# A hybrid diffusion block on one core: the 16-to-32 step of block inversions on 32x32 tiles, and delta-net decays from two single-pass products

## The chip, the cores and the metric

The kernel runs on one NeuronCore of a Trainium2 chip. A core has TensorE (PE in the profile; PEld is its loading of weights), VectorE (DVE), ScalarE (ACT), GpSimd (POOL) and SyncE (SP, which here issues DMAs). Each engine works through its own queue of instructions in order and waits on semaphores for the others. Matrix products read SBUF and write PSUM, which has eight banks here divided into pools. The metric is the device time of one execution in microseconds (us); lower is better. The time before is the median of three runs.

## The reference, cut to what matters

One layer of a backbone: 256 latent tokens and 256 context tokens, 2048 channels. Modulated RMSNorm, one wide input projection, then two token mixers side by side, RWKV-7 and a chunked gated DeltaNet, each in both directions; their outputs are projected, gated, merged and added; then a SwiGLU feed-forward part. Two pieces bear on the change. The delta net computes in each chunk of 64 tokens

```python
gc = jnp.cumsum(chunks(g), axis=-1)
diff = gc[..., :, None] - gc[..., None, :]
decay = jnp.where(incl, jnp.exp(jnp.where(incl, diff, 0.0)), 0.0)
lmat = jnp.where(strict, jnp.einsum('nbhik,nbhjk->nbhij', kb, kc) * decay, 0.0)
sol = lax.linalg.triangular_solve(lmat, rhs, left_side=True, lower=True, unit_diagonal=True)
q_dec = qc * jnp.exp(gc)[..., None]
```

so that each head and direction needs a matrix of exponentials of differences of cumulated log decays, the exponentials of the cumulated decays themselves, and the solution of a unit triangular system of 64 rows. The RWKV recurrence is written in the reference as a scan over single tokens; the kernel computes it in chunks of 64 too, which leads to triangular matrices of the same kind.

## The kernel before, in words

The program has four parts. First, a start phase: norms of both token sets, part of the modulation, and the low-rank projections. Second, the middle, which holds both mixers. Third, the projections of both branches and the merge; fourth, the feed-forward part and the final norm. Parts three and four are long rows of weight products. A weight product in full precision is made of three fp32r (single-pass) products of split operands: ScalarE casts a weight tile to fp32r (`whi`), VectorE subtracts to get the rest (`wlo`), and TensorE multiplies high by high, high by low and low by high. These three are the groups `mm<-hxh,whi`, `mm<-hxl,whi` and `mm<-hxh,wlo`.

The middle isn't written out in order. A planner, `Weave`, takes generators (one per piece of work: `prepare`, `grams`, `inverse`, `values`, `scan` for each of 8 pairs of RWKV heads; `features`, `tokens`, `decays`, `head_grams`, `head_inverse`, `head_scan` for each of 8 delta-net heads; `products` for the input projections; `ada_rest` for further modulation), gives each operation a cost (`Lane`), and emits the operations in the order in which its own clock lets them start, by rank among those that are ready. Named marks (`yield "scan", p - 1` and the like) hold a piece back until another has been reached. The emitted order is then each engine's queue order. `products` has a low rank and fills TensorE where nothing else is ready. Since every operation is issued from one line, L142 stands for all of the middle in the profile, and groups are told apart by tile names.

An inversion (`invert`) works on `nu` unit triangular blocks of 64x64 per half of the partitions: 16 for an RWKV pair (8 chunks, two directions) and 8 for a delta-net head. The blocks go through DRAM (`scr`, `tscr`) into a layout in which VectorE inverts all 16x16 diagonal blocks by substitution. They come back as `T0` and, transposed, `Tx`. Then two merging steps follow on TensorE: 16 to 32 and 32 to 64. The 16-to-32 step goes direction by direction: a product of 64x64 tiles with half the columns (32) into the one bank of the pool `pi`, a masked copy by VectorE (`Qm`, with the mask `qmask`), a second product of the same form, an addition into `T0`, and a transpose to `Tx`. The 32-to-64 step (`quads`) already uses 32x32 tiles. RWKV's `scan` of a pair and the delta net's `head_scan` wait for their inversion.

`decays` makes, per head and direction, an operand `gm` (a triangle of ones times the log decays, 128x512, by VectorE), multiplies it in fp32 by the triangle `aft` (512 columns) and by `ones` (256 columns), and takes exponentials on ScalarE: `Ed`, which GpSimd masks, and `eq`, which VectorE multiplies into `Qe`. `gm` lies in one place of a hand-divided `arena`.

Of the kernel before, what the change touches and what calls it, by code (L numbers as in the profile page):

```python
# [18 lines left out]
P = 128  # L19
# [18 lines left out]
for _name, _w in (("ident", 128), ("ones", 128), ("bd64", 128), ("rmask", 256),  # L38
                  ("qmask", 64), ("tri", 256), ("aft", 256), ("q4", 4), ("q2", 2),
                  ("eps", 1), ("gneps", 1)):  # L40
    _C[_name] = (_n, _n + _w)
    _n += _w
NC_COLS = _n

# [10 lines left out]
def const_array():  # L55
# [12 lines left out]
    rb, cb = s // 16, t // 16  # L68
    same = (rb // 2) == (cb // 2)
    even = np.arange(64) // 16 % 2 == 0  # L70
    put("qmask", np.concatenate([(same & (rb % 2 == 1))[:, even], (same & (rb % 2 == 0))[:, ~even]], 1))
# [39 lines left out]
class Lane:  # L111
# [5 lines left out]
    def __getattr__(self, name):  # L117

        def op(out, *a, **k):
# [148 lines left out]
def emit(ctx: ExitStack, tc, A, out, dbg=None):  # L268
# [17 lines left out]

    C = cst.tile([P, NC_COLS], F32, name="C")
    Q.dma_start(C, A["consts"])
# [12 lines left out]
    ident, ones, bd64 = c_("ident"), c_("ones"), c_("bd64")  # L301
    rmask = c_("rmask").rearrange("p (d k) -> p d k", d=2)
    qmask = c_("qmask").rearrange("p (d a c) -> p d a c", d=2, a=2)
    tri = c_("tri").rearrange("p (d t) -> p d t", d=2)
    aft = c_("aft").rearrange("p (d t) -> p d t", d=2)
# [23 lines left out]
    zero = cst.tile([P, 130], F32, name="zero")  # L329
    G.memset(zero, 0.0)  # L330
# [74 lines left out]
    with tc.tile_pool(name="p0", bufs=1) as p0, \  # L405
            tc.manual_schedule(engines={mybir.EngineType.PE, mybir.EngineType.DVE, mybir.EngineType.Activation,
                                        mybir.EngineType.SP}):
        modc = p0.tile([P, 32], F32, name="modc")
# [143 lines left out]
    def invert(pool, Lt, parts, nu, which, full, fill):  # L552
# [52 lines left out]
        def half(t, d):  # L605
            ax = "p u"[:2 * len(t.shape) - 3]
            return t.rearrange(f"{ax} (a b c) -> {ax} a b c", a=2, b=2)[..., d, :]

        def mm(ps, d, lhs, rhs):
            return [e.matmul(ps[64 * h:64 * h + 64, 32 * i:32 * i + 32], lhs(h, h2 * d + i), rhs(h, h2 * d + i),  # L610
                             start=True, stop=True) for i in range(h2) for h in range(2)]
# [1087 lines left out]
```

## Time and profile before

| | us |
|---|---|
| median of three runs (2334.98 to 2337.48) | 2336.01 |
| the profiled execution | 2348.77 |
| its span, first to last instruction | 2346.7 |
| TensorE busy (95%) | 2223.8 |
| VectorE busy (66%) | 1557.2 |
| ScalarE busy (45%) | 1047.9 |
| GpSimd busy (5%) | 113.5 |

Busy time says that instructions were in flight; matmuls overlap, so a busy TensorE can still be waiting between them, and the distance from one start to the next is the better measure of what a matmul costs. A row of groups gives the line, the engine, the operation, out<-in by tile names, the shapes, the count, then busy us and mean ns of one, then the idle time before it and what ended that. A row of the timeline gives start and length in us; x32 means that 32 records were merged. An fp32 matmul leaves two records, an fp32r matmul one. Rows of busy time by stretch give busy us and count for each engine, then the clock granted to TensorE (1.00 is full), the share of the DMA engines and the rate.

### The profile page before, as it was taken

To read this page: it belongs to the slowest core of one execution; us is meant where nothing else is said; L and a number is where in the kernel's file an instruction comes from. 1 tells how busy PE (TensorE), PEld (TensorE's weight loads), DVE (VectorE), ACT (ScalarE), POOL (GpSimd) and SP (SyncE) were. 2 spreads that over 40 slices of the span, in tenths; PEclk is the share of its full clock that TensorE was granted. 3 is DMA by queue.
4 is the path that set the end of the run, shared out by engine and by line. 5 is a ranking of instruction groups with operands and counts; after the bars stand their busy time and mean duration, and the time that the engine had idled before them with its cause. 6 is when DMAs were issued, how large, how long until landed. Compare 5 with 4: busy or idle time off the path is not lost. (4 is left out here: it accounts for less than half of the span.)

```text
span 2346.7 us, 51488 instructions
## 1 busy us (share of the span) xinstructions
PE 2223.8 (95%) x21368; PEld 1951.7 (83%) x21368; DVE 1557.2 (66%) x3237; ACT 1047.9 (45%) x1863; POOL 113.5 (5%) x183
## 2 busy tenths in 40 slices
PE   7988999999999999999798999999999999999998
PEld 4767677778788777776677989999999999999997
DVE  3447588778986489889878645765666556545454
ACT  3246454544355544344234346544444444444443
POOL 0000000000000011111111003000000000000000
PEclk9999999999999999999789999999999999999999
DMA  9956454434344256657466565663777776566665
GB/s 377 397 148 189 152 134 102 111 83 117 100 109 133 85 172 207 189 167 217 145 191 194 182 219 180 209 214 107 239 233 234 234 238 218 187 185 194 191 191 165
DMA packets 232570, 430.58 MB, mean 183 GB/s; under 512 B 114832, under 2 KB 130064, under 8 KB 227984
## 3 DMA queue, kind: packets, MB, share of 16 engines
q1 hardware_dynamic: 204688, 351.78, 48.4%
q0 software_dynamic: 13824, 50.34, 7.0%
q10 hardware_dynamic: 13824, 25.17, 3.5%
q8 instruction: 167, 2.74, 0.5%
q14 instruction: 67, 0.55, 0.1%
HBM read 401.45 MB, written 25.77 MB: 182 GB/s over the span
## 5 line engine op out<-in xcount | busy, mean ns | idle before, releaser
L357 DVE TENSOR_TENSOR wlo<-wraw,whi 128x1024 fp32r<-128x1024 f32 x328 | 393.5, 1200 | 351.1 <-ACT whi L356 348.2
L356 ACT CAST whi<-wraw 128x1024 fp32r<-128x1024 f32 x328 | 337.7, 1030 | 472.8 <-PE mm L367 413.8
L142 PE MATMUL mm<-hxh,wlo 128*128 128x256 f32 (+1 forms) x1376 | 468.3, 340 | 9.9 <-DVE wlo L142 9.7
L142 PE MATMUL mm<-hxh,whi 128*128 128x256 f32 (+1 forms) x1376 | 469.0, 341 | 3.4 <-ACT whi L142 3.3
L142 PE MATMUL mm<-hxl,whi 128*128 128x256 f32 (+1 forms) x1376 | 468.3, 340 | 0.0
L368 PE MATMUL mm<-hfh,wlo 128*128 128x256 f32 x1344 | 377.1, 281 | 0.4 <-DVE wlo L357 0.4
L366 PE MATMUL mm<-hfh,whi 128*128 128x256 f32 x1344 | 376.5, 280 | 0.0
L367 PE MATMUL mm<-hfl,whi 128*128 128x256 f32 x1344 | 375.2, 279 | 0.0
L142 PEld LDWEIGHTS mm<-hxh,wlo 128*128 128x128 f32 x1376 | 265.6, 193 | 39.4 <-DVE wlo L142 13.0
L142 PEld LDWEIGHTS mm<-hxh,whi 128*128 128x128 f32 x1376 | 265.6, 193 | 31.5 <-issue 6.5
L142 PEld LDWEIGHTS mm<-hxl,whi 128*128 128x128 f32 x1376 | 265.8, 193 | 27.2 <-issue 6.1
L142 DVE TENSOR_TENSOR wlo<-wraw,whi 128x512 fp32r<-128x512 f32 x344 | 236.2, 690 | 62.7 <-ACT whi L142 60.0
L142 ACT CAST whi<-wraw 128x512 fp32r<-128x512 f32 x344 | 205.8, 618 | 112.1 <-PE mm L142 88.9
L366 PEld LDWEIGHTS mm<-hfh,whi 128*128 128x128 f32 x1344 | 253.4, 189 | 0.0
L368 PEld LDWEIGHTS mm<-hfh,wlo 128*128 128x128 f32 x1344 | 252.8, 188 | 0.6 <-DVE wlo L357 0.6
L367 PEld LDWEIGHTS mm<-hfl,whi 128*128 128x128 f32 x1344 | 253.2, 188 | 0.0
L142 DVE TENSOR_TENSOR arena<-arena 128x28 f32<-128x28 f32 (+13 forms) x538 | 132.0, 247 | 32.1 <-DMA arena<-scr 20.4
L366 PE MATMUL mm<-za,whi 128*128 128x256 f32 x512 | 141.8, 277 | 0.0
L367 PE MATMUL mm<-za,whi 128*128 128x256 f32 x512 | 141.7, 277 | 0.0
L368 PE MATMUL mm<-za,wlo 128*128 128x256 f32 x512 | 141.6, 277 | 0.0
L142 DVE SCALAR_TENSOR_TENSOR aw<-aw,ck 128x512 f32<-128x512 f32 x180 | 131.2, 739 | 5.1 <-DMA aw<-ada_rest 4.4
L368 PEld LDWEIGHTS mm<-za,wlo 128*128 128x128 f32 x512 | 96.2, 188 | 0.0
(311 smaller groups left out, 3924.5 us busy)
## 6 DMA issues: line engine op xcount, KB each, us to landing
wraw<-w SPq DMA_DIRECT2D x172, 512.0 KB, 4.3
wraw<-wgu SPq DMA_DIRECT2D x168, 512.0 KB, 4.5
aw<-ada_rest POOLq DMA_DIRECT2D x96, 512.0 KB, 4.7
aw<-ada_first SPq DMA_DIRECT2D x32, 1024.0 KB, 11.5
wraw<-wdn SPq DMA_DIRECT2D x64, 448.0 KB, 3.7
wraw<-wout SPq DMA_DIRECT2D x32, 512.0 KB, 4.7
aw<-ada_gt ACTq DMA_DIRECT2D x64, 256.0 KB, 5.0
wraw<-wdn SPq DMA_DIRECT2D x32, 512.0 KB, 3.6
```

The source lines that it names most:

```text
L142: return Op(self, cost, lambda: getattr(self.engine, name)(out, *a, **k), split)
L356: S.copy(hi[:, c, :M], raw[:, c, :M])
L357: V.tensor_sub(lo[:, c, :M], raw[:, c, :M], hi[:, c, :M].bitcast(F32))
L366: E.matmul(ps, hi, Xh[:, k, :n], start=first and i == 0, stop=False)
L367: E.matmul(ps, hi, Xl[:, k, :n], start=False, stop=False)
L368: E.matmul(ps, lo, Xh[:, k, :n], start=False, stop=last and i == len(wt) - 1)
```

## The change

It has two parts and what they need.

The 16-to-32 step is done for both directions together. Each 32x32 diagonal block is handled by its own tile: a product with the 16 columns that matter, a multiply-add by VectorE per direction (`low16` selects rows, `eye16` adds the identity), a second product of the same form, eight copies into `T0` (four by VectorE, four by ScalarE), and one transpose of all of `T0`. The planner's cost of a matmul with fewer than 64 rows goes from 0.024 to 0.009 or 0.0125.

The log decays are split into an fp32r part `ghi` and the rest `glo`. ScalarE, not VectorE, builds two operands from the triangle, each by four activations with a per-partition scale (128x128). Each product by `aft` and by `ones` becomes two accumulating fp32r products, so `aft` and `ones` are kept as fp32r (`CR`), loaded by a DMA of their own and cast by ScalarE at the start. The exponential is written straight into `Qe` and multiplied there. The operands take the pool places `k` and `kkn` of the RWKV stage, which for that leave the arena; `eq`, `gm`, `q3` and `hb` lose their own places, and `zero` moves to the start phase's pool. Head 0 waits for the inversion of pair 6.

```diff
-                    cost = 0.024
+                    cost = 0.009 if n <= 16 else 0.0125
...
+        cr = p0.tile([P, NR_COLS], F32, name="cr")
+        Q.dma_start(cr, A["consts"][:, NC_COLS - NR_COLS:])
+        S.copy(CR, cr)
...
-        Qm = xt[:, :32 * nu].rearrange("p (u c) -> p u c", c=32)
+        fours = [(h, u, 32 * b, slice(64 * h + 32 * b, 64 * h + 32 * b + 32)) for u in range(nu) for h in range(2) for b in range(2)]
+        Qm = xt[:, :16 * nu].rearrange("p (u c) -> p u c", c=16)
+        ps = yield pib
+        pv = ps[:, 0:32 * nu].rearrange("p (k u c) -> p k u c", k=2, c=16)
+        yield [e.matmul(pv[r, 0, u], Lt(h, u)[b:b + 32, b:b + 32], T0[r, u, b + 16 * (u // h2):b + 16 * (u // h2) + 16],
+                        start=True, stop=True) for h, u, b, r in fours]
         for d in range(2):
-            T0d = half(T0[:, us[d]], d)
-            ps = yield pib
-            yield mm(ps, d, Lt, lambda h, u: half(N_(h, u), d))
-            pv = ps[:, 0:32 * h2].rearrange("p (i a c) -> p i a c", a=2, c=16)
-            yield v.tensor_mul(Qm[:, us[d]].rearrange("p i (a c) -> p i a c", a=2), pv,
-                               qmask[:, d].unsqueeze(1).to_broadcast([P, h2, 2, 16]))
-            yield mm(ps, d, Nt_, lambda h, u: Qm[64 * h:64 * h + 64, u, :])
-            yield v.tensor_add(T0d, pv, T0d)
-            weave.release(pib)
-            yield v.transpose(Tx[:, us[d]], T0[:, us[d]])
+            yield v.scalar_tensor_tensor(Qm[:, us[d]], pv[:, 0, us[d]], low16[:, d:d + 1],
+                                         eye16[:, d].unsqueeze(1).to_broadcast([P, h2, 16]), ALU.mult, ALU.add)
+        yield [e.matmul(pv[r, 1, u], Tx[r, u, b:b + 32], Qm[r, u, :], start=True, stop=True) for h, u, b, r in fours]
+        for h in range(2):
+            yield [(s.copy if h else v.tensor_copy)(T0[r, us[d], b + 16 * d:b + 16 * d + 16], pv[r, 1, us[d]])
+                   for d in range(2) for b in (0, 32) for r in (slice(64 * h + b, 64 * h + b + 32),)]
+        weave.release(pib)
+        yield v.transpose(Tx, T0)
...
+        yield s.copy(ghi, gtok)
+        yield v.tensor_sub(glo, gtok, ghi.bitcast(F32))
...
+        else:
+            yield "inverse", NPAIR - 2
...
-            gm = gs.tile([P, 4, P], F32, tag="gm", name="gm")
-            yield v.tensor_mul(gm, tri[:, d].unsqueeze(1).to_broadcast([P, 4, P]),
-                               gtok[:, :, col:col + 1].to_broadcast([P, 4, P]))
-            gf = gm.rearrange("p b c -> p (b c)")
+            gm = [rpool.tile([P, 512], F32R, tag=t, name="gm") for t in ("k", "kkn")]
+            for t, g2 in zip(gm, (ghi.bitcast(F32), glo)):
+                for b in range(4):
+                    yield s.activation(t[:, P * b:P * b + P], tri[:, d], AF.Identity, scale=g2[:, b, col:col + 1])
             ps = yield pab
-            yield e.matmul(ps, aft[:, d], gf, start=True, stop=True)
+            yield [e.matmul(ps, aftr[:, d], t, start=i == 0, stop=i == 1) for i, t in enumerate(gm)]
...
-            yield e.matmul(ps[:, :T], ones, gf[:, 0:T], start=True, stop=True)
-            eq = gs.tile([P, T], F32, tag="eq", name="eq")
-            yield s.activation(eq, ps[:, :T], AF.Exp)
+            yield [e.matmul(ps[:, :T], onesr, t[:, 0:T], start=i == 0, stop=i == 1) for i, t in enumerate(gm)]
+            qe = o["Qe"][:, d]
+            yield s.activation(qe, ps[:, :T], AF.Exp)
             weave.release(pab)
-            yield v.tensor_mul(o["Qe"][:, d], o["q"], eq)
+            yield v.tensor_mul(qe, qe, o["q"])
...
-        q3 = gs.tile([P, 4, 64], F32, tag="q3", name="q3")
+        q3 = gs.tile([P, 4, 64], F32, tag="XT", name="q3")
```

More of the change, by code (lines that the diff above doesn't have):

```diff
@@ L43 @@
 NC_COLS = _n
+NR_COLS = 384
 _P = {}
@@ L674, in emit @@
     arp = ent(tc.tile_pool(name="arp", bufs=1))
-    arena = arp.tile([P, 9544], F32, name="arena")
-    rplaces = (("k", 512, 1), ("r", T, 1), ("t1", 512, 1), ("kd0", 512, 1), ("kd1", 512, 1), ("kkn", 512, 1), ("sg", 512, 1),
+    arena = arp.tile([P, 8520], F32, name="arena")
+    rplaces = (("r", T, 1), ("t1", 512, 1), ("kd0", 512, 1), ("kd1", 512, 1), ("sg", 512, 1),
                ("ic", 512, 2), ("ei", 520, 1), ("LT", 1024, 2), ("XT", 512, 1), ("prod", 64, 1),
@@ L1130, in emit @@
     nbtok = cst.tile([P, 4, 16], F32, name="nbtok")
+    ghi = cst.tile([P, 4, 16], F32R, name="ghi")
+    glo = cst.tile([P, 4, 16], F32, name="glo")
     al = cst.tile([P, 1], F32, name="al")
@@ L1169, in begin @@
         yield [e.matmul(ps[:, T + 64 * i + 32 * d:T + 64 * i + 32 * d + 32], m[:, d], gtok[:, :, 8 * d:8 * d + 8], start=True, stop=True)
-               for d in range(2) for i, m in enumerate((tri, aft))] + [e.matmul(ps[:, 3 * P:3 * P + 64], ones, gtok, start=True, stop=True)]
+               for d in range(2) for i, m in enumerate((tri, aftr.bitcast(F32)))] + [e.matmul(ps[:, 3 * P:3 * P + 64], ones, gtok, start=True, stop=True)]
         for i, t in enumerate((egc, eta)):
```

48 lines of the change are left out of this document (23 added, 25 removed).

## The prediction

> **What bounds the kernel now.** I read the page's busy line and slices first, then busy time by stretch, the waits of TensorE, the order of time around one inversion and one decay step, and last the groups of instructions by shape.
>
> ```profile
> PE 2223.8 (95%) x21368; PEld 1951.7 (83%) x21368; DVE 1557.2 (66%) x3237; ACT 1047.9 (45%) x1863; POOL 113.5 (5%) x183
> DVE  3447588778986489889878645765666556545454
> ACT  3246454544355544344234346544444444444443
> ```
>
> The shares are averages over unlike stages; the digits show VectorE at 8 or 9 tenths only in the middle. The middle (some 165 to 1390 us) holds both token mixers, and all of the change but its constants lies there.
>
> ```profile
> core 0: us, PE busy (x) PEld busy (x) DVE busy (x) ACT busy (x) POOL busy (x), PEclk, DMA share, GB/s
> 400.00:800.00 400.00, 397.07 (x5220) 312.66 (x5220) 312.60 (x778) 194.93 (x483) 11.24 (x30) 1.00 0.40 107
> 800.00:1000.00 200.00, 186.06 (x1490) 152.36 (x1489) 162.40 (x395) 87.81 (x164) 28.98 (x43) 0.97 0.59 179
> 1000.00:1200.00 200.00, 177.17 (x1380) 138.11 (x1380) 171.37 (x420) 80.53 (x148) 33.48 (x54) 0.90 0.62 186
> 1200.00:1390.00 190.00, 171.99 (x1755) 157.59 (x1755) 134.44 (x349) 78.21 (x162) 11.12 (x17) 0.97 0.59 179
> 1390.00:2346.00 956.00, 929.72 (x7878) 924.12 (x7876) 535.55 (x713) 428.69 (x558) 21.23 (x16) 0.99 0.65 204
> ```
>
> Columns are the stretch, its length, busy time and count of each engine, and the granted clock. In the RWKV stage (400 to 800) TensorE is busy 397 of 400 us at full clock, VectorE 78%, ScalarE 49%. In the delta-net stage (1000 to 1200) TensorE has 89% at a clock of 0.90 and VectorE 86%: two engines near their limit. After 1390 only weight products run (956 us); the change leaves them alone.
>
> ```profile
> PE pa L142 <- DVE arena L142: 0.8, 2, 0.5
> PE mm L142 <- DVE wlo L142: 0.4, 1, 0.4
> PE pa L142 <- ACT arena L142: 5.5, 5, 1.9
> PE pa L142 <- DVE arena L142: 4.0, 2, 3.3
> PE pi L142 <- DMA T<-tscr: 3.3, 1, 3.3
> ```
>
> These are TensorE's waits, total us, times, longest: two rows of 400 to 800, where nothing holds it longer than 0.8 us in all, and three of 1000 to 1200, where the decay products (pa) wait for ScalarE or VectorE. So TensorE time is worth nearly its full amount in the RWKV stage and part of it later.
>
> **Inversion step: the matmuls.** Before, each inversion runs four sets in a row (two directions, two products each), each set on 64x64 tiles, 32 columns wide. Afterwards there are two sets for both directions, of 32x32 tiles and 16 columns. One fp32 matmul is two records in the trace: the RWKV set of 16 matmuls shows as x32.
>
> ```profile
> 622.80 1.12 PE L142 MATMUL pi<-arena 64*64 64x32 f32 x32
> 623.75 0.43 PE L142 MATMUL s<-R,Tx 64*64 64x64 f32 x8
> 625.39 1.12 PE L142 MATMUL pi<-arena,Tx 64*64 64x32 f32 x32
> 626.44 0.45 PE L142 MATMUL s<-VX,KB 128*64 128x64 f32 x8
> 632.40 0.76 PE L142 MATMUL pi<-Tx,arena 32*32 32x32 f32 x64 [0.45 <-DVE arena L142]
> 633.09 0.45 PE L142 MATMUL s<-R,Tx 64*64 64x64 f32 x8
> 1013.31 0.66 PE L142 MATMUL pi<-T,LT 64*64 64x32 f32 x16 [1.00 <-DVE T L142]
> 1024.46 0.45 PE L142 MATMUL pi<-Tx,qo 32*32 32x32 f32 x32
> 1024.84 0.71 PE L142 MATMUL pa<-arena 128*128 128x128 f32 x4
> ```
>
> From start to next start an old RWKV set holds TensorE 0.95 us (622.80 to 623.75) and 1.05 us (625.39 to 626.44), about 1.0. The later 32x32 step, which is kept, is the nearest row for the new form: 64 records in 0.69 us (632.40 to 633.09), some 11 ns a record against 31. A new RWKV set has 64 matmuls, 128 records, half as wide. Upper end: each costs what a 32-column one costs, 2 x 0.69 = 1.38 us. Lower end: half of that, 0.69 us, if the columns count. I take 1.0, between them, since the same tile form is known and only its width is not. So 4 x 1.0 goes and 2 x 1.0 comes: 2.0 us for each of 8 pairs, 16 us (10 to 21).
>
> The Trainium skill ("TensorEngine Tiling (Array Packing)", Performance Considerations, Instruction Overhead) says that a matmul with one column takes as long as one with 60. By it the upper end holds and the RWKV term is 8 x (4.0 - 2.76) = 10 us; no run shown has 16 columns, so the trace neither agrees nor disagrees.
>
> In a delta-net head a set is half as long: the old one lasts 0.66 us, some 0.55 us without the tail that overlaps what follows. A new one has 64 records: 0.69 at most, 0.38 us at least (the x32 run at 1024.46, next start 1024.84); I take 0.55. Four go and two come: 1.1 us for each of 8 heads, 9 us (6.5 to 11.5).
>
> **Inversion step: the other engines.**
>
> ```profile
> L142 DVE TENSOR_TENSOR arena<-pi,C 128x256 f32<-128x256 f32 x16 | 6.7, 417 | 3.6 <-PE pi L142 3.5
> L142 DVE TENSOR_TENSOR arena<-pi,arena 128x256 f32<-128x256 f32 x16 | 6.7, 419 | 5.5 <-PE pi L142 5.4
> L142 DVE STREAM_TRANSPOSE Tx<-arena 128x512 f32<-128x512 f32 x24 | 16.9, 704 | 21.0 <-DMA arena<-tscr 20.8
> L142 DVE COPY Tx<-pi 32x256 f32<-32x256 f32 x16 | 6.6, 412 | 3.1 <-PE pi L142 2.8
> L142 ACT COPY R<-s 128x128 f32<-128x128 f32 x64 | 17.0, 265 | 86.8 <-PE s L142 86.5
> ```
>
> VectorE gives up 2 x 0.417, 2 x 0.419 and 2 x 0.704, 3.1 us a pair. It gets two 128x128 multiply-adds and four 32x128 copies, some 0.3 us each (scaled down from the 256-wide rows), and one transpose of twice the width, at most 1.4: 3.2 us. The same; a head likewise. ScalarE gets four copies, 1.1 us a pair by the 265 ns row. Its share of 49% covers that; uncovered it would be under 10 us over 8 pairs. There are two round trips between TensorE and VectorE instead of four, which shortens the inversion's latency; I give that nothing, since the next scan is queued behind its own predecessor.
>
> **Decays: the products.** Per head and direction an fp32 product of 512 columns and one of 256 each become two single-pass products that accumulate.
>
> ```profile
> 1035.25 0.40 PE L142 MATMUL mm<-hxl,whi 128*128 128x512 f32 x1
> 1035.48 0.40 PE L142 MATMUL mm<-hxh,wlo 128*128 128x512 f32 x1
> 1035.72 0.28 PE L142 MATMUL mm<-hxh,whi 128*128 128x256 f32 x1
> 1035.84 0.28 PE L142 MATMUL mm<-hxl,whi 128*128 128x256 f32 x1
> 1036.07 1.02 PE L142 MATMUL pa<-arena,C 128*128 128x512 f32 x2
> 1036.93 1.05 PE L142 MATMUL s<-TF,keg 128*128 128x128 f32 x8
> ```
>
> The fp32 one holds TensorE 0.86 us (1036.07 to 1036.93), and half as wide 0.43 us as an estimate. A single pass of 512 takes 0.23 us (1035.25 to 1035.48), of 256 0.12 (1035.72 to 1035.84). 1.29 becomes 2 x 0.23 + 2 x 0.12 = 0.70; 16 times 0.6 is 9.5 us off TensorE.
>
> **Decays: the operand moves to ScalarE.**
>
> ```profile
> L142 DVE TENSOR_TENSOR arena<-C,gtok 128x512 f32<-128x512 f32 x16 | 10.8, 674 | 0.1
> L142 ACT ACTIVATE arena<-arena 128x512 f32<-128x512 f32 x56 | 34.1, 628 | 19.4 <-DVE arena L142 12.1 <-issue 6.7
> L142 ACT ACTIVATE arena<-arena 128x256 f32<-128x256 f32 x32 | 13.1, 416 | 17.4 <-DVE arena L142 16.8
> L142 ACT ACTIVATE arena<-mm,om 128x512 f32<-128x512 f32 x16 | 11.0, 687 | 20.9 <-PE mm L142 11.8 <-PE pa L368 8.1 <-PE pi L142 0.9
> ```
>
> VectorE loses 16 x 0.674, 10.8 us, in the stage where it is near its limit. ScalarE gets 8 instructions of 128x128 for each, 128 in all. Their price lies between the 265 ns copy and 0.37 us: 628 to 416 ns for half the width gives 310 ns at 128, and the row with a per-partition scale adds 59 (687 against 628). I take 0.3 with overlap: a burst of 2.4 us and 38 us in all (34 to 47), beside 247 us now busy of 590 from 800 to 1390. The sum takes this as hidden; uncovered it is the first rival's price. Behind each burst in ScalarE's queue stand the weight casts that feed TensorE; the exponentials of the decays wait for it as well. The new head-0 wait for pair 6's inversion costs nothing, because the same routine already waits for pair 6's scan, which follows that inversion.
>
> **The rest.** The second constants DMA and its cast stand ahead of the first square; they carry bytes that the first DMA drops, so 0 to 1 us (one issue, one cast); I take 0.5. The two splits of the log decays are tiny. Tile moves (q3, t2, hb, k, kkn, zero) keep count and size; nothing is late on their account unless a new reader lies nearer, and the old places were also one deep. The planner's lower price for small matmuls moves the written order everywhere. TensorE idles 3 + 14 + 23 + 18 = 58 us from 400 to 1390 (by the stretches); another order could give back or add a sixth, 10 us; I take 0.
>
> **The sum.** TensorE loses 16 us in the RWKV stage; at 99% busy I count three quarters, 12, since the scan's own chain of steps and VectorE at 78% take the rest. In the delta-net stage it loses 9 + 9.5 and VectorE 10.8; both are coupled through in-order queues and the clock falls when TensorE idles, so I count half of TensorE's 18.5 and nothing twice: 10. Less 0.5: 21.5, say 22 us. The profiled execution took 2348.8 us (span 2346.7 and 2.1 around it) and would take 2326.8; that is 12.8 above the median of 2336.0, so the median goes to 2314.
>
> **Rivals.**
> First, slower: the ScalarE bursts hold back weight casts. Against it speak a ScalarE half idle and VectorE's relief; for it, that it has one in-order queue and TensorE's largest wait in 1000 to 1200 is already on ScalarE. If each burst costs TensorE 2.1 us, 16 cost 34; less the 22 that gives +12, 2348. It decides from 22/16 = 1.4 us a burst. Here the Trainium skill ("ScalarE: Activation LUTs", Rules for kernel authors) advises the other way: multiplications on VectorE, not ScalarE.
> Second, the gain is hidden: the scan chain and VectorE set the pace and TensorE merely idles more. The 86% of VectorE speaks for it, the 397 of 400 us against. 2334, between 2327 and 2341.
> Third, all of it counts: 16 + 18.5 off, and five from order and VectorE's relief, 39.5 in all: 2297.
> Fourth, small records cost the same whatever their tile: at the 31 ns of the 64x64 sets a new RWKV set takes 4.0 us, two 8.0 against 4.0, +32 over the pairs, +14 over the heads, -9.5; at six tenths +22, 2358. The 11 ns record speaks plainly against it. The Trainium skill ("TensorE: Matmul & The Clock Gate", Part 1) names a floor of about 25 ns from start to start; by that the RWKV stage would lose 8 x (6.4 - 4.0) = 19 us, and the trace's 11 ns disagrees.
>
> **How the numbers follow.** Forecast (2302 to 2327) 0.42, casts held back 0.18, hidden 0.16, all of it 0.18, record price 0.03, else 0.03. The range from 2292 to 2346 leaves out the far end of the third and the upper parts of the first and the fourth. Within 0.2% (4.7 us), about what a measurement can tell from no change, lie parts of the hidden case, 0.07; faster are forecast, third and the hidden case's low end, 0.66; slower the rest, 0.27.
>
> **What would show it.** Right: the new sets as runs of 32x32, 16 columns, at 0.7 to 1.4 us for 128 records; decay products under 0.75 us together; scans of successive pairs some 1.5 us closer; ScalarE up by 40 to 55 us; the weight products after the middle starting some 22 us sooner and otherwise unchanged. Wrong: waits of mm products for whi casts grown by 20 us or more, more idle TensorE at a lower clock in 800 to 1390, or new waits in the RWKV stage.

## The result: no difference, and the profile after

The changed kernel took 2340.32 us (median of 12 runs, 2331.42 to 2352.76); the kernel before, beside it on the same chip, 2341.06 us. The ratio is 1.001, with a 95% interval of 0.9994 to 1.0025: no difference that this kernel's measurement can show. The forecast was 2314. The profiled execution has a span of 2342.3 us, against 2346.7.

The busy line and two rows of slices of the changed kernel's page:

```profile
PE 2200.5 (94%) x22904; PEld 1940.9 (83%) x22904; DVE 1555.0 (66%) x3238; ACT 1101.7 (47%) x2058; POOL 110.6 (5%) x183
DVE  3447588888877568889788745765565655555554
ACT  3246454454455555454455546544444444444443
```

TensorE's busy time fell by 23 us, VectorE's by 2, and ScalarE's rose by 54; the time stayed. (Busy time is only a rough count of work: the kernel before's own instructions, written in two other orders further down, e4 and g6, have 2208.0 and 2202.5 us on TensorE.) Busy time by stretch of the changed kernel says where the time stayed:

```profile
core 0: us, PE busy (x) PEld busy (x) DVE busy (x) ACT busy (x) POOL busy (x), PEclk, DMA share, GB/s
400.00:800.00 400.00, 389.37 (x5871) 306.74 (x5869) 309.61 (x780) 200.36 (x503) 10.13 (x30) 0.97 0.40 108
800.00:1000.00 200.00, 180.20 (x1655) 147.31 (x1656) 157.48 (x376) 103.04 (x227) 26.15 (x40) 0.96 0.54 166
1000.00:1200.00 200.00, 168.51 (x1580) 136.29 (x1579) 171.43 (x426) 100.15 (x212) 32.35 (x52) 0.90 0.59 183
1200.00:1390.00 190.00, 175.43 (x1993) 162.45 (x1992) 141.54 (x371) 90.72 (x203) 13.18 (x21) 0.97 0.64 197
1390.00:2342.00 952.00, 929.23 (x7879) 923.88 (x7877) 535.52 (x714) 428.14 (x555) 21.35 (x16) 0.99 0.62 204
```

From 400 to 1390 TensorE now idles 10.6 + 19.8 + 31.5 + 14.6 = 76.5 us, where before it idled 58 (the four rows in the prediction). So 19 us of busy time became 19 us of idle time, and the middle ended at the same moment. The weight products after 1390 are unchanged (929.2 and 929.7 us busy).

Two marks of the middle, from the views of the tiles R (one copy per RWKV scan step) and Vn (one per delta-net scan step), first and last start at the end of the numbers. The kernel before:

```profile
L142 ACT COPY R<-s x64: 248/266/270, 281.1 to 831.1; 128x128 f32<-128x128 f32 x64
...
L142 DVE TENSOR_SCALAR Vn<-s,btok x64: 328/336/352, 906.4 to 1383.7; 128x128 f32<-128x128 f32 x64
```

The changed kernel:

```profile
L143 ACT COPY R<-s x64: 247/265/272, 277.7 to 846.9; 128x128 f32<-128x128 f32 x64
...
L143 DVE TENSOR_SCALAR Vn<-s,btok x64: 327/338/352, 927.5 to 1384.1; 128x128 f32<-128x128 f32 x64
```

The RWKV scans take 569 us instead of 550; from the last of them to the last delta-net step it takes 537 instead of 553. The RWKV stage, where I expected 12 us of gain, lost 19, and the delta-net stage gained 15. The two are not independent, since weight products fill both and what is done in one isn't left for the other.

One thing more changed in the RWKV stage: from 400 to 800 the granted clock is 0.97, where it was 1.00. The same 50 us before and after, then three rows of TensorE in the changed kernel:

```profile
550.00:600.00 50.00, 50.00 (x670) 39.61 (x663) 39.99 (x96) 26.55 (x66) 1.51 (x4) 1.00 0.45 120
...
550.00:600.00 50.00, 47.67 (x811) 39.51 (x808) 41.12 (x87) 23.49 (x59) 1.87 (x6) 0.90 0.39 108
...
557.55 0.59 PE L143 MATMUL pi<-arena 32*32 32x16 f32 x48
560.48 0.41 PE L143 MATMUL pi<-arena 32*32 32x16 f32 x16 [2.33 <-issue]
...
564.79 2.18 PE L143 MATMUL pi<-arena,Tx 32*32 32x16 f32 x128
```

TensorE stops for 2.33 us inside a new set, and from 560.5 to 570.5 its granted clock is 0.50; from 765.5 to 779 it is 0.50 again. Half the clock over these 24 us is worth at most 12 us as an estimate, of the 19 that the stage lost. The kernel before has no such stretch between 400 and 800.

The new sets and, at 492.97, the kept 32x32 step, in the order of time on TensorE:

```profile
482.31 0.73 PE L143 MATMUL pi<-arena 32*32 32x16 f32 x64
483.45 0.73 PE L143 MATMUL pi<-arena 32*32 32x16 f32 x64 [0.42 <-DVE arena L143]
484.11 0.50 PE L143 MATMUL mm<-hxh,wlo 128*128 128x512 f32 x1
...
486.21 1.59 PE L143 MATMUL pi<-arena,Tx 32*32 32x16 f32 x128
487.74 0.45 PE L143 MATMUL s<-R,Tx 64*64 64x64 f32 x8
...
492.97 0.75 PE L143 MATMUL pi<-arena 32*32 32x32 f32 x64
493.65 0.50 PE L143 MATMUL mm<-hxl,whi 128*128 128x512 f32 x1
```

From one start to the next, 64 records of 16 columns take 0.66 us (483.45 to 484.11) and 64 records of 32 columns 0.68 us (492.97 to 493.65). Half the columns save nothing. Two new sets hold TensorE 1.80 us (482.31 to 484.11, a wait of 0.42 in it) and 1.53 us, together 3.3 against four old ones at about 1.0.

### The profile page after: what moved, and what is told of

Same layout as the page of the kernel before. It is cut to its first block, busy times and chain, and to the rows that moved or that the text cites. A ratio compares the mean times of both kernels' runs of the same rounds, so it can differ in the third digit from the quotient of the medians.

```text
span 2342.3 us, 54751 instructions
## 1 busy us (share of the span) xinstructions
PE 2200.5 (94%) x22904; PEld 1940.9 (83%) x22904; DVE 1555.0 (66%) x3238; ACT 1101.7 (47%) x2058; POOL 110.6 (5%) x183
## 4 chain that ended last, share of the span: by engine, by line
PE 62%; DVE 11%; DMA 6%; ACT 4%; issue 2%; SPq 0%; ACTq 0%; DVEq 0%
PE mm L143 16%; PE mm L371 12%; PE mm L369 12%; PE mm L370 12%; PE s L143 4%; DVE arena L143 4%; PE pa L143 3%; PE pi L143 2%; DVE aw L143 2%; DVE wlo L143 2%; DMA wr<-wgu 1%; DMA tscr<-arena 1%; ACT arena L143 1%; DMA Tx<-tscr 1%; DVE wlo L360 1%
## 5 line engine op out<-in xcount | busy, mean ns | idle before, releaser
L143 PEld LDWEIGHTS mm<-hxh,whi 128*128 128x128 f32 x1376 | 266.8, 194 | 36.2 <-ACT whi L143 10.8
L143 DVE TENSOR_TENSOR arena<-arena 128x39 f32<-128x39 f32 (+17 forms) x522 | 120.9, 234 | 23.8 <-DMA arena<-scr 8.0
L370 PEld LDWEIGHTS mm<-za,whi 128*128 128x128 f32 x512 | 96.1, 188 | 0.0
```

Source lines behind the costliest of these rows:

```text
L143: return Op(self, cost, lambda: getattr(self.engine, name)(out, *a, **k), split)
L370: E.matmul(ps, hi, Xl[:, k, :n], start=False, stop=False)
```

## The experiments

Medians in us, ratios to the kernel before on the same chip with 95% intervals; the RWKV column is first to last copy R, then the granted clock from 400 to 800, the start of the last step Vn, and how long before the end of the span TensorE's last 6000 records begin, all of them late weight products that no run edits.

| kernel | median | ratio | RWKV | clock | last Vn | late |
|---|---|---|---|---|---|---|
| the kernel before | 2341.06 | 1 | 550 | 1.00 | 1383.7 | 709 |
| the changed kernel | 2340.32 | 1.001 (0.9994 to 1.0025) | 569 | 0.97 | 1384.1 | 710 |
| e1_price | 2331.46 | 0.9966 (0.9952 to 0.998) | 561 | 0.98 | 1372.0 | 712 |
| e2_inversion_only | 2345.98 | 1.0039 (1.0018 to 1.0059) | 568 | 0.99 | 1381.8 | 713 |
| e3_decays_only | 2342.00 | 1.0008 (0.9992 to 1.0023) | 553 | 1.00 | 1370.3 | 715 |
| e4_price_only | 2335.42 | 0.998 (0.9966 to 0.9994) | 556 | 1.00 | 1382.4 | 708 |
| f1_decays_same_order | 2350.30 | 1.004 (1.0017 to 1.0064) | 552 | 1.00 | 1379.8 | 719 |
| f2_inversion_same_order | 2369.76 | 1.0111 (1.0074 to 1.0147) | 563 | 0.97 | 1391.4 | 718 |
| f3_both_same_order | 2358.96 | 1.0072 (1.0047 to 1.0097) | 568 | 0.97 | 1396.7 | 711 |
| f4_tensor_relief | 2344.98 | 1.0009 (0.9984 to 1.0034) | 550 | 1.00 | 1372.8 | 707 |
| g1_tensor_less | 2335.05 | 0.9972 (0.9956 to 0.9987) | 548 | 1.00 | 1371.2 | 708 |
| g2_vector_less | 2323.98 | 0.9928 (0.9908 to 0.9949) | 544 | 1.00 | 1369.1 | 710 |
| g3_true_prices | 2338.16 | 0.9983 (0.9962 to 1.0003) | 560 | 0.98 | 1375.7 | 715 |
| g4_inversion_true_price | 2338.59 | 0.9994 (0.9977 to 1.0011) | 559 | 0.97 | 1387.3 | 714 |
| g6_before_price_215 | 2314.02 | 0.9893 (0.9859 to 0.9927) | 544 | 1.00 | 1356.9 | 707 |
| g7_price_18 | 2341.91 | 1.001 (0.9989 to 1.0031) | 555 | 0.99 | 1372.8 | 711 |
| h1_copies_vector | 2374.35 | 1.0155 (1.013 to 1.0181) | 577 | 0.95 | 1408.3 | 714 |
| h2_by_direction | 2345.42 | 1.0021 (1.0003 to 1.0039) | 553 | 1.00 | 1373.5 | 712 |
| j1_decays_price_215 | 2335.26 | 0.997 (0.9949 to 0.9991) | 542 | 1.00 | 1361.8 | 720 |
| j2_by_direction_planned | 2335.27 | 0.9963 (0.994 to 0.9985) | 560 | 1.00 | 1381.7 | 712 |

The marks, the clock and the late column come from one execution each, and the time that follows the last Vn lies between 946 and 972 us in these profiles, so a mark alone is good to some 15 us; what is called faster or slower goes by the ratios.

### The parts one at a time, planned anew

The change has three parts: the inversion, the decays, and the planner's price of a small matmul, which was lowered from 0.024 us to 0.009 or 0.0125. The measured price is 0.66 us for 32 matmuls, 21 ns. My first theory was that the wrong price spoils the order; the rival, that a part itself costs time.

e1: the changed kernel, with the measured price.

```diff
-                    cost = 0.009 if n <= 16 else 0.0125
+                    cost = 0.0215
```

> The changed kernel, with the planner's price of a matmul with fewer than 64 rows set to 0.0215 us, what the trace of the kernel before gives (64 records of 32 matmuls in 0.69 us), instead of 0.009 and 0.0125. Price theory: the RWKV stage of the changed kernel grew by some 16 us (last scan step 831 to 847 us) because the order was planned with half the true cost of the small matmuls; with the true price the last scan step comes back to 831 or earlier and the time falls to about 2325. Form theory: the new step itself costs the time (new waits), and the stage stays near 847, the time near 2340. Theory that something else bounds: time within 0.2% of 2340 whatever the stage marks do.

e2: the kernel before with the new inversion and the new price. e3: the changed kernel with the old inversion and the old price, so the decays alone. e4: the kernel before with nothing but the new price.

```diff
-                    cost = 0.024
+                    cost = 0.009 if n <= 16 else 0.0125
```

> The kernel before with the new inversion step and the new price only; decays as before. Price theory and form theory: last RWKV scan step near 847, the delta-net stage as long as before (553 us from there to the last step), time about 2350 to 2355. Theory that something else bounds: within 0.2% of the kernel before.

> The changed kernel with the old inversion step and the old price: only the decays (and constants, places) are changed. Price theory and form theory: RWKV stage as before (831), delta-net stage some 10 to 15 us shorter, time about 2326 to 2330. If ScalarE's bursts held TensorE back more than the products save, the delta-net stage is longer and the time above 2345. Theory that something else bounds: within 0.2% of the kernel before.

> The kernel before with nothing changed but the planner's price for matmuls with fewer than 64 rows (0.024 to 0.0125 us for those of the 32-to-64 step): the same instructions in another order. Price theory: last RWKV scan step later than 831 by 3 to 10 us and time up by as much. Form theory and the theory that something else bounds: marks and time unchanged within 0.2%.

The right price gave 8 us (e1), which spoke for the theory. But the wrong price on the kernel before did not cost, it gave 5 us (e4). The inversion alone costs 9 us here (14 beside e4, which has the same price) and the decays alone give nothing. Each of these kernels also has another written order, so they do not separate the parts from the order.

### The parts in the old order

These runs keep the kernel before's written order: every new instruction is issued at the place of one that it replaces. f1 puts the eight activations at the place of the old VectorE product, and the pairs of fp32r products at the place of the fp32 ones:

```diff
-            yield v.tensor_mul(gm, tri[:, d].unsqueeze(1).to_broadcast([P, 4, P]),
-                               gtok[:, :, col:col + 1].to_broadcast([P, 4, P]))
+            yield Op(v, v.fixed + v.each * 512, operands)
...
-            yield e.matmul(ps, aft[:, d], gf, start=True, stop=True)
+            yield Op(e, 0.0054 + 0.00167 * 512, lambda ps=ps, gm=gm, d=d: [
+                E.matmul(ps, aftr[:, d], t, start=i == 0, stop=i == 1) for i, t in enumerate(gm)])
```

f2 puts the whole joint inversion at the first direction's places and leaves the second's empty; f3 is both.

```diff
+            if d == 0:
...
+                calls = (set1, mask, set2, back, lambda: V.transpose(Tx, T0))
+            else:
+                calls = (lambda i: None, lambda: None, lambda i: None, lambda: None, lambda: None)
```

> The kernel before with the new decays alone, but written at the very places of the old instructions: the planner sees the old costs, so everything else stands in the order of before. The eight operand instructions stand on ScalarE where the one VectorE instruction was planned. If the changed parts were worth what TensorE and VectorE save (9.5 and 10.8 us, half of it counted): 5 to 10 us below the kernel before. If the ScalarE bursts hold TensorE as long as the products save: within 0.2% of it.

> The kernel before with the new inversion step alone, its instructions at the places of the first direction's old ones and nothing at the second direction's; the rest in the order of before. The traces give 0.6 us of TensorE saved for each pair and 0.75 for each head, 11 us. If TensorE's time counts in full in the RWKV stage: 6 to 11 us below the kernel before. If the order alone made the kernel with the new inversion (2346) slow, this one must not be slower than before; if the form of the step did, it is 5 us slower here too.

> Both parts of the change in the order of before. Order theory (the changed kernel lost to its newly planned order what its parts gained): 10 to 20 us below the kernel before, 2322 to 2330. Form theory: about the same as before and as the changed kernel, 2340.

In a fixed order neither part gains: by the ratios the decays cost 9 us, the inversion 26, both 17; f1 and f3 lie above both of their forecasts. But not all of this lies in the mixers. Near the end, where the same weight products run in every kernel, the kernel before and then f1 get this far in 200 us:

```profile
2100.00:2300.00 200.00, 200.00 (x1751) 200.00 (x1750) 100.21 (x105) 89.17 (x106) 0.00 (x0) 1.00 0.67 192
...
2100.00:2300.00 200.00, 200.00 (x1699) 200.00 (x1698) 98.23 (x103) 86.25 (x103) 0.00 (x0) 1.00 0.64 186
```

At the same clock and with TensorE always busy, f1 starts 3% fewer records. Its late column is 719 us against 709, while its last Vn comes no later than before (1379.8 and 1383.7): so far as one execution each can tell, the decays' 9 us lie behind the mixers, and inside them the part neither cost nor gained. f2 has 718 there, so some 10 of its 26 us are of the same kind; f3 has 711, which fits that both parts together seem cheaper than one. The six kernels without either part have 707 to 710, the eight with one part 712 to 720, the six with both 710 to 715. What slows the late products is not known, and no run tests it.

The waits of TensorE and VectorE in f2 from 400 to 800 (total us, times, longest) show what the inversion itself costs:

```profile
PE pi L620 <- issue: 7.5, 5, 2.5
DVE arena L632 <- PE pi L620: 11.9, 6, 3.0
DVE Tx L633 <- ACT arena L632: 4.3, 6, 1.2
```

L620 is the second set, L632 the copies into `T0`, L633 the transpose. VectorE stands at its copies for the end of a second set that now holds TensorE 2.6 us (median of the eight pairs, stops included), where the one it replaces held it 1.05, and then for ScalarE's half of the copies; all that follows in VectorE's queue waits too. In the kernel before, the rows of this kind, which lump all steps of the inversion, were:

```profile
PE pi L142 <- issue: 0.5, 1, 0.5
...
DVE arena L142 <- PE pi L142: 6.7, 7, 2.7
```

Two runs ask what in f2 does it. h1 gives ScalarE's four copies to VectorE; h2 does the same 32x32 tiles with 16 columns, each direction by itself, at its own old places.

```diff
-                                (S.copy if h else V.tensor_copy)(T0[r, us[q], b + 16 * q:b + 16 * q + 16], pv[r, 1, us[q]])
+                                V.tensor_copy(T0[r, us[q], b + 16 * q:b + 16 * q + 16], pv[r, 1, us[q]])
```

```diff
-                    for h, u, b, r in fours[4 * i:4 * i + 4]:
+                for h, u, b, r in fours[d][2 * i:2 * i + 2]:
```

> The run of the inversion step alone in the old order (2370, RWKV scans 563 us from the first to the last step, against 550 before) with one difference: all eight copies back by VectorE, none by ScalarE. If ScalarE's copies, standing in its queue until TensorE's second set is done, hold up the scan's own copies behind them: RWKV scans back to 550 to 555 us and 2345 to 2355. If not: 560 us or more and 2365 to 2375.

> The same base, the new tiles and columns, but each direction by itself at the places of the old direction's instructions: four sets of 32 matmuls, one multiply-add, four copies and one half transpose each. If joining both directions in one place is what makes the queues wait: RWKV scans 548 to 553 us and 2335 to 2342. If the tile form or the copies do it: 558 us or more and 2355 or above.

Not ScalarE's copies: without them h1 is no faster than f2 (1.0155 against 1.0111), though its VectorE then has 17 us more to do (1579.2 against 1562.4 busy). Joining the directions is: h2 is 5 us over the kernel before, f2 26. Of these 21 us 6 are late products (712 and 718), the other 15 lie before them. The same waits in h2:

```profile
PE pi L620 <- issue: 1.4, 1, 1.4
DVE arena L630 <- PE pi L620: 2.9, 2, 2.3
DVE Tx L142 <- ACT arena L630: 2.5, 7, 0.6
```

The three rows shrink from 23.7 to 6.8 us together, and the clock from 400 to 800 is 1.00 again. And yet h2 is not faster than the kernel before.

### How much a saved microsecond of an engine is worth

The prediction counted three quarters of TensorE's saving in the RWKV stage. f4, g1 and g2 take work away from the kernel before in its own order, in the products of the gates. f4 makes their third product 128 columns wide instead of 256 (640 matmuls). g1 does not issue every second of those products, 320 of them, 37 us of TensorE by starts 0.115 us apart. g2 lets VectorE subtract only half of each weight tile for them, and TensorE uses `whi` in place of the missing half.

```diff
+                    if what == "g" and j == 2:
+                        op.call = lambda ps=ps, w=w, x=x, k=k: E.matmul(ps[:, :P], w[:, k % 8], x[:, k, :P], start=False, stop=k == KT - 1)
```

```diff
+                    if what == "g" and j == 2 and k % 2 == 0:
+                        op.call = lambda: None
```

```diff
+                if gate:
+                    g2 = slice(k, k + 2)
+                    op.call = lambda lo=lo, raw=raw, hi=hi, g2=g2: V.tensor_sub(lo[:, g2], raw[:, g2], hi[:, g2].bitcast(F32))
```

> The kernel before in its own order, but the third product of each of the 640 k-steps of the 40 gate projections has 128 columns instead of 256 (so half of the low part of these gates is left out): 640 times 0.058 us, 37 us less work for TensorE, some 20 of it in the RWKV stage, and nothing else changed. If TensorE's time sets the end, 30 us or more of it come off (2310 or below); if chains and VectorE set it, under 10 us.

> The kernel before in its own order; every second third-product of the 40 gate projections is not issued (so the low parts of half of these weights are left out): 320 matmuls of some 0.116 us, 37 us of TensorE work, weight loads included, 20 of it in the RWKV stage. The shortened products of the run before took nothing off, because the weight load of the next matmul then set the pace (three matmuls still took 0.35 us). If TensorE sets the end: 25 us or more off, 2315 or below, RWKV stage 15 us or more shorter. If chains through in-order queues set it: under 10 us.

> The kernel before in its own order; in the casts for the 40 gate projections VectorE subtracts only half the columns (256 instead of 512; the third products of the other half read the high part, so half of these low parts are left out): 160 times 0.27 us, 43 us less for VectorE, some 23 in the RWKV stage. If VectorE sets the end: 25 us or more off. If TensorE or chains do: under 10 us.

f4 tests nothing, because TensorE got no relief from it. The short product lets the next one start after 61 ns, but that one then takes 170 ns to the following start instead of 114 (medians), so a triple still takes 0.35 us; its group has this row:

```profile
L1090 PEld LDWEIGHTS mm<-hxh,wlo x640: 186/189/337, 138.0 to 1369.8; 128*128 128x128 f32 x160
```

Each product loads its own weights, and a load lasts 189 ns (median) here and 188 for the products of 256 columns in the kernel before. That the loads set the pace was not tested apart.

g1 is the clear one. 37 us less for TensorE gave 6.6 us (3 to 10 by the interval): 0.18 of it. Busy time from 400 to 800 in g1:

```profile
400.00:800.00 400.00, 392.49 (x5121) 305.16 (x5120) 310.81 (x773) 194.96 (x484) 10.79 (x28) 1.00 0.39 108
```

TensorE did 99 fewer records there, some 11 us, and is still busy 392 of 400 us, 5 less than before; the rest of its matmuls were in flight for longer. In g2 the other engine loses work, 160 subtractions that shrink from 681 to 416 ns, 42 us by these medians of the tile's view of the kernel before and of g2:

```profile
L142 DVE TENSOR_TENSOR wlo<-wraw,whi x344: 623/681/1961, 137.6 to 1376.3; 128x512 fp32r<-128x512 f32 x172
```

```profile
L1038 DVE TENSOR_TENSOR wlo<-wraw,whi x160: 375/416/1711, 137.3 to 1361.5; 128x256 fp32r<-128x256 f32 x160
```

They gave 17 us (12 to 22), 0.40 of it, between the two forecasts. g2 also frees TensorE from some waits for `wlo`, but in the same views these fell by 2 us only (9.7 to 7.8). The work taken away lies all over the middle, so both figures are means over its stages: a microsecond of VectorE, busy 78% of the RWKV stage, was worth about twice one of TensorE, busy 99% of it, and neither its full amount.

### The order

g3 gives the planner the measured prices of both the small matmuls and the activations (0.30 us for what it priced at 0.17); g4 is e2 with the measured matmul price; g7 is the changed kernel at 0.018; g6 is the kernel before, its instructions untouched, at 0.0215.

```diff
+                if name == "activation" and n == P and not isinstance(k.get("scale", 1.0), float):
+                    cost = 0.30
```

```diff
-                    cost = 0.024
+                    cost = 0.0215
```

> The changed kernel with two planner prices set to what traces show: small matmuls 0.0215 us (as in the run that gave 2331) and the 128x128 activations with a per-partition scale 0.30 us instead of 0.17. If TensorE's 17 us of waiting for these operands comes from planning them too short: those waits fall under 8 us and the time to 2322 to 2328. If it comes from ScalarE's queue itself: waits as before and 2331 within 0.2%.

> The kernel before with the new inversion step alone, planned with 0.0215 us for small matmuls (the run with 0.009 and 0.0125 gave 2346). If the wrong price was what cost time there: 2330 to 2337. If the form of the step costs it: 2344 to 2350.

> The changed kernel planned with 0.018 us for small matmuls, between its own 0.009 and 0.0125 (2340) and the 0.0215 that gave 2331. If the true price is the cause: 2331 to 2337. If any new order is a draw of some 10 us: anything from 2330 to 2350, and no trend with the price.

> The kernel before planned with 0.0215 us instead of 0.024 for the 32-to-64 step's matmuls, nothing else: a second sample of what another order alone does to the same instructions (0.0125 gave 2335 against 2340). If prices near the truth matter: within 0.2% of the kernel before. If an order is a draw: off by up to 0.4% either way.

The price theory fell here. With both prices right the changed kernel takes 2338 (g3), with one right 2331 (e1), at a price between 2342 (g7): no trend; g4, at 2339, lies between its two forecasts. And the kernel before, by a change of 0.0025 us in one cost of its planner, went from 2341 to 2314 (25 us by the ratio), far outside both forecasts and the fastest of all kernels here. Its row from 1000 to 1200 and its last step:

```profile
1000.00:1200.00 200.00, 179.44 (x1455) 142.33 (x1453) 184.12 (x451) 83.21 (x157) 34.92 (x56) 0.96 0.66 196
```

```profile
L142 DVE TENSOR_SCALAR Vn<-s,btok x64: 223/338/352, 894.1 to 1356.9; 128x128 f32<-128x128 f32 x64
```

The same instructions, and VectorE gets through 184 us of work in the 200 instead of 171. The granted clock is 0.96 there instead of 0.90. Over the whole span it is 0.984 to 0.989 in g6's four executions and 0.974 to 0.982 in the 19 of the kernel before beside them, so the clock is a rival. It does not cover all: the one execution of the kernel before at 0.985, among those beside f1, took 2326.0, and g6 at 0.984 and 0.985 took 2313.8 and 2318.1. Whether the clock makes the rest of the time, or the waits make the clock, was not shown.

Beside all this scatter two things are steady. At each price the kernel with neither part is not beaten: 2341 against 2342 at 0.024 (e3), 2335 against 2346 and 2340 at 0.009 and 0.0125 (e4; e2, changed), 2314 against 2331 to 2339 at 0.0215 (g6; e1, g4, j1, j2). And beside a kernel of the same price or order the joined step lengthens the RWKV stage every time: 563 and 568 us against 550 and 552 in the old order (f2, f3; before, f1), 568 and 569 against 556 (e2, changed; e4), 559 and 561 against 544 and 542 (g4, e1; g6, j1). Its granted clock from 400 to 800 is 0.95 to 0.99 in all nine kernels with the joined step, 1.00 in the eleven others.

Two last runs: whether that price is good for the decays alone as well, and whether the inversion by direction (h2's form, without its old order) helps the planned change.

```diff
-                    cost = 0.024
+                    cost = 0.0215
```

```diff
+            yield [e.matmul(pv[r, 0, u - h2 * d], Lt(h, u)[b:b + 32, b:b + 32], T0[r, u, b + 16 * d:b + 16 * d + 16],
+                            start=True, stop=True) for h, u, b, r in fours[d]]
```

> The changed kernel with the old inversion (the decays' part alone), planned at the price 0.0215 at which the kernel before took 2314.02. If that price's order is good for a reason that outlives small edits, this lies at 2305 to 2325. If each order is a draw of its own, it lies with the decays alone at the old price (2342.0) within the spread of the other orders, 2330 to 2350; my theory, the draw, expects 2340.

> The changed kernel with its inversion done direction by direction on 32x32 tiles, planned at the price 0.0215. If joining the two directions is what cost the change its gain, as the runs in the old order say (28 us lost joined, 5 us apart), this is faster than the changed kernel by 10 us or more, 2330 or less. If the planner's order decides more than that, it lies anywhere from 2325 to 2350; I expect 2332.

j1 takes 2335, not 2314. Yet the middle kept most of the gain: its last Vn starts at 1361.8, g6's at 1356.9 and the kernel before's at 1383.7. What j1 lacks against g6 lies mostly behind it, in late products of 720 us against 707. So j1 does not show that g6's order was a mere draw. j2, also 2335, is under the changed kernel by 5 us in the medians and 11 in the ratios, but it also has another price; beside e1, which has the same price and the joined step, it gains nothing (0.9963 and 0.9966), and its RWKV stage takes 560 us as e1's 561. So in the planned orders the joining is not shown to cost anything, and the step on 32x32 tiles lengthens the stage by direction too. What it is in g6's order that helps stays open.

## Why the prediction was wrong

**The bound.** "TensorE time is worth nearly its full amount in the RWKV stage" is the step that failed first. It read 397 busy of 400 us and waits of under a microsecond as an engine without slack. g1 shows the slack: 37 us less work, 6.6 us less time, 0.18 over the middle where I counted 0.75 for this stage. A busy TensorE here is one with a matmul in flight. In place of the 12 us that I counted as gain for the RWKV stage, the joined step lengthened it by 12 to 19 us in each of the comparisons above. That the pace is set by VectorE, ScalarE and TensorE meeting in their queues in the written order is my reading; g2's 0.40 and g6's 25 us speak for it from two sides, and no run shows it alone. This was my second rival (the gain is hidden, 2327 to 2341), to which I gave 0.16 since I weighed the 397 of 400 us above VectorE's load. Of my signs of being wrong, new waits in the RWKV stage came; the lower clock came in that stage too, and not from 800 to 1390, where I looked for it. (In the sum, half of 18.5 is 9.3, not 10; that moves the forecast by less than 1 us.)

**The inversion's matmuls, 16 + 9 us.** The mechanism was right (two sets for four) and the size was off. I took 1.0 us a new set between 0.69 and 1.38; measured are 1.53 and 1.80 from start to next start in the rows above, 1.76 as the median of all 16, stops included. So a pair saves some 0.6 to 0.7 us, not 2.0, and a head 0.75 (two sets of 0.79 for four of 0.585 as medians), not 1.1: 11 us together, not 25. With every long stop counted it is less: all these sets hold TensorE 57 us instead of 61. Two things made it so. The columns do not count: the 64 records take 0.66 us with 16 columns and 0.68 with 32. The Trainium skill ("TensorEngine Tiling (Array Packing)", Performance Considerations, Instruction Overhead) has a matmul of one column take as long as one of 60. The trace agrees for 16 and 32 columns; with equal times for both, the RWKV term was at its low end of 10 us from the start. And many sets now stop on their way: at 483.45 for VectorE, 0.42 us, at 560.48 for 2.33 us in which the profile shows nothing that TensorE waited for. My upper end of 1.38 us left stops out; the four shortest of the 16 took 1.19 us. The fourth rival fell as expected, at 10 ns a record. The Trainium skill ("TensorE: Matmul & The Clock Gate", Part 1) names a floor of about 25 ns from start to start. The trace shows no such floor for these tiles.

**"The same" on VectorE, and latency at nothing.** The total came out nearly the same: VectorE's busy time is 1555.0 after 1557.2, with its 10.8 us of operands gone; e2, with the inversion alone, has 1561.4. So the inversion's pieces cost it some 4 to 9 us more than before. What I did not price is that they come in one chain: set, two multiply-adds, set, copies on two engines, one transpose of double width. I credited that as two round trips fewer. In the old order the step costs 26 us joined and 5 apart (f2, h2), some 16 and 2 without the late products; in the orders planned at 0.0215 joined and apart are alike (e1, j2).

**Decays, the operand on ScalarE.** The price held. Its groups in the changed kernel:

```profile
L143 ACT ACTIVATE gm<-C,glo 128x128 fp32r<-128x128 f32 x64 | 22.2, 391 | 0.0
L143 ACT ACTIVATE gm<-C,ghi 128x128 fp32r<-128x128 f32 x64 | 21.2, 393 | 0.1
```

That is 43.4 us in all, between my 34 and 47, and ScalarE's total rose by 54 where I said 40 to 55. "Taken as hidden" held in part only. A burst in order of time on ScalarE:

```profile
1046.69 1.28 ACT L143 ACTIVATE gm<-C,ghi 128x128 fp32r<-128x128 f32 x4
1047.87 0.68 ACT L143 ACTIVATE gm<-C,glo 128x128 fp32r<-128x128 f32 x2
1048.60 0.60 ACT L143 ACTIVATE arena<-s 128x512 f32<-128x512 f32 x1
1049.10 0.39 ACT L143 ACTIVATE gm<-C,glo 128x128 fp32r<-128x128 f32 x1
1049.39 0.61 ACT L143 CAST whi<-wraw 128x512 fp32r<-128x512 f32 x1
1049.90 0.40 ACT L143 ACTIVATE gm<-C,glo 128x128 fp32r<-128x128 f32 x1
```

The four of `ghi` take 1.18 us to the next start, 0.3 each as taken, but the burst isn't closed: other work stands in it and it lasts 3.6 us. TensorE sat idle for its end, in the tile's view of the changed kernel:

```profile
  ACT gm L143: 17.3, 9
```

In e1, the same kernel with another price, it was this:

```profile
  ACT gm L143: 0.8, 3
```

The first rival was therefore right in kind: the operands do hold TensorE, though not by late weight casts but directly, at the products that need them; the waits of TensorE from 1000 to 1200 in the changed kernel:

```profile
PE pa L143 <- ACT gm L143: 4.5, 1, 4.5
...
PE mm L143 <- ACT whi L143: 1.2, 1, 1.2
```

Its size depends on the order. e1 shows that 16 us of this wait can go, and e1 is 9 us faster than the changed kernel; that the wait is the cause of the 9 was not shown, since e1 has another order everywhere, and g3, with 0.6 us of the wait, is 2 us faster by the medians.

**The order, "I take 0", 10 us either way.** Far too narrow. Three orders of the very same instructions took 2341, 2335 and 2314 (the kernel before, e4, g6), and the changed kernel's instructions took 2331 to 2342 in four orders. The spread is as large as the whole gain I worked out, so a sum of instruction costs could not carry a chance of 0.66 for faster. The changed kernel against the kernel before is a draw of two orders too: that it came out at no difference, and not some 10 us to either side, is in part luck.

**What held.** TensorE's work fell, though less than the 34.5 us that were counted (some 11 by the sets as measured and the 9.5 of the decays, whose pairs of products show their 0.23 and 0.12 us a pass where nothing holds them); the later weight products did not move; the second constants DMA is not seen in the time, as the marks begin at 277.7 against 281.1; and the range, 2292 to 2346, took in 2340, though the reason I gave for it was wrong.

## What to carry to other kernels

Before a saving is counted, ask what an engine's microsecond is worth at that place, and measure it by not issuing some of its work in the same order: here a microsecond of TensorE was worth 0.18 and one of VectorE 0.40. Where a planner writes the order, compare parts in the old order and plan several orders of each version, since a cost changed by 0.0025 us moved the same instructions by 25 us, as much as the dearer part of this change in the old order. Look where in the span a difference lies before it is put down to the edited part: f1's 9 us lie in late products that the edit does not touch. Joining two short steps of different directions into one long step saves instructions but puts a longer chain at one place of each in-order queue; in the old order that cost 21 us (15 before the late products), in the one pair planned alike (e1, j2) nothing that shows.

## What the runs showed of the hardware

Fp32 matmuls on 32x32 tiles take about 10 ns a record in runs of 64 records, with 16 columns as with 32 (0.66 and 0.68 us). In a row of fp32r products that each load their own 128x128 weights, 128 instead of 256 columns in every third product saved nothing: a triple took 0.35 us as before. After a stop of TensorE of 2.33 us its granted clock was 0.50 for 10 us. The same late weight products ran at 1751 and at 1699 records in 200 us in two kernels that differ elsewhere in the program, both at clock 1.00. A scaled activation of 128x128 written as fp32r lasts 391 ns and follows the one before it by 0.3 us.
